# The last 512 gate columns of a decoder trunk: weight panels split ahead and kept, products token tile by token tile, the second tile in two halves

## Chip, cores, metric

One core of a Trainium2 chip. The time is device microseconds of one execution; several executions are timed and their median is given. One execution is also profiled, with a record of every instruction and DMA; its own time is given beside its span (first to last instruction). All durations below come from that profile.

## The reference

One layer of a decoder trunk for 256 tokens and a width of 2048, all in float32: a mixer (pooling and a recurrent time mix), a squared-ReLU MLP, and a gated embedding, then a final norm. The change touches the end alone:

```python
x = x + jnp.square(jax.nn.relu(h2 @ w_ffn_up[i])) @ w_ffn_down[i]
gate = jax.nn.sigmoid(rms_norm(x, ple_norm[i]) @ w_ple_gate[i])   # 2048 x 2048
x = x + gate * (p[i] @ w_ple_proj[i])                             # p: 256 wide
...
return rms_norm(x, final_norm)
```

## The kernel before, in words

**Numbers.** A float32 matrix product is made of three products of rounded operands: every operand v is split into a high part h (v rounded to float32r by a copy on ACT) and a low part l = v - h (a subtraction on DVE), and h·h + h·l + l·h is accumulated in PSUM. So weights can't go from memory straight to PE. A *panel* is 256 rows by 512 columns of a weight, 512 KB in SBUF as [128, 1024]. `load_raw` (L120) loads it on SP's DMA queue into one of three buffers `raw`; `split_w` (L125) makes `wh` (two ACT copies of 512 columns, L131; three buffers) and `wl` (one DVE subtraction, L132; two buffers). Then PE runs 12 matmuls with it: two row blocks, two token tiles of 128 tokens (tt = 0, 1), three products each (L153, L154, L155 in `prod_toks`). The activations are the stationary operand, the weights the moving one.

**Queues.** Every engine runs its instructions in one order, which the framework's scheduler sets from the order in the source and from priorities: the splits carry a high priority, so that they come as early in ACT's and DVE's order as their buffers let them. A load waits for its `raw` buffer (the split of three panels before), `wh` for PE's last matmul on the panel three before, `wl` for the one two before.

**The stages at the end**, all with `gemm_toks` (L172), which takes two PSUM banks from a ring of four (`mm_bank`), one for each token tile:
- the second half of the FFN's down product, tiles `d`, 4 column blocks of 16 panels. After each block DVE adds the result to the residual x, one operation for each token tile (L874), and PE transposes the new 512 columns into the banks `h3t` (L815), from which ACT and DVE make the split operand `h` of the gate product (L821, L822);
- the projection of p, tiles `pp`, 4 blocks of one panel each; ACT copies every bank to SBUF (L890). Beside it ACT sums the squares of x for the norm (L194, `junk`);
- the gate product, tiles `gt`, 4 column blocks n of 8 panels. After each block, for each token tile: sigmoid from the bank on ACT (L903), times pp (L908) and plus x (L909) on DVE, square with accumulation on ACT (L910), times the final norm's weights on DVE (L912, not in the last block);
- after the last block a sum of the accumulators (L914), root (L203) and reciprocal (L204) for both token tiles at once, then the scaling of x: ACT 768 columns (L919), DVE 768 (L920) and 512 (L921), and one store on ACT's queue (L922, 384 KB) and one on SP's (L923, 640 KB) for each token tile. A tiny activation `warm` (L906) makes ACT load the root's table early.

The FFN's activations stand in eight buffers `y` of [128, 2048], free once the last down block has used them.

## Time and profile before

| | |
|---|---|
| median of 3 runs (lowest to highest) | 1243.79 us (1243.69 to 1247.84) |
| the profiled execution, its span | 1242.95 us, 1241.2 us |
| granted TensorE clock, mean | 0.99 |
| ACT copy of 128x512 in a split (L131), gate panels | 624 ns |
| DVE subtraction of 128x1024 (L132), gate panels | 1224 ns |
| load of a gate panel, issue to landing, median | 3.5 us |
| PE's first and last matmul of the gate product | 1140 to 1227 us |

The rows of the profile read: start, duration, engine, source line, operation, output<-inputs, partitions x elements, and in brackets the idle time of the engine before it and what ended it. Rows of groups end in the busy time and the mean ns of one. A matmul's printed duration is from its issue to its end in a pipeline, so that consecutive ones overlap; the distance of their starts is what PE spends on each.

### The profile page before, as it was taken

The numbers are of one execution on the slowest core, as the hardware profiler recorded it, in microseconds if no ns is written. First come the engines' busy times: TensorE is split into PE (matmuls) and PEld (weight loads), VectorE is DVE, ScalarE is ACT, GpSimd is POOL, SyncE is SP. The second block draws the span as 40 slices with busy tenths as digits, with TensorE's granted clock in tenths as the row PEclk, the third lists the DMA queues.
The fourth block names the chain that finished last, engine by engine and source line by source line (L and its number), as shares of the span: only waits on it lengthen the run. The fifth ranks groups of instructions, "written<-read, shape, count | busy, mean of one in ns | idle before, by whom it ended". The sixth has DMA issues, their size and how long they took to land. (4 is left out here: it accounts for less than half of the span.)

```text
span 1241.2 us, 18647 instructions
## 1 busy us (share of the span) xinstructions
PE 1208.0 (97%) x7230; PEld 1039.7 (84%) x7230; DVE 751.0 (61%) x919; ACT 631.4 (51%) x1164; POOL 9.8 (1%) x58
## 2 busy tenths in 40 slices
PE   6999999999999999999999999999999999999995
PEld 4999898989888888888888888888888888888884
DVE  2678978875665566666554444656656455445564
ACT  6755555464455545555444444445544444446553
POOL 2000000000000000000000000000000000000000
PEclk9999999999999999999999999999999999999998
DMA  6453433222556656666666666655656655655663
GB/s 273 166 167 130 153 121 137 69 96 92 192 190 182 211 189 192 191 191 189 192 198 188 197 192 189 187 187 185 188 187 188 198 187 188 189 188 192 193 198 118
DMA packets 59944, 218.99 MB, mean 176 GB/s; under 512 B 6672, under 2 KB 6928, under 8 KB 59216
## 3 DMA queue, kind: packets, MB, share of 16 engines
q1 hardware_dynamic: 59424, 216.95, 54.5%
q8 instruction: 56, 0.92, 0.3%
q10 hardware_dynamic: 432, 0.86, 0.2%
q14 instruction: 32, 0.26, 0.1%
HBM read 215.68 MB, written 2.10 MB: 175 GB/s over the span
## 5 line engine op out<-in xcount | busy, mean ns | idle before, releaser
L794 PE MATMUL u_w<-h,wh_u 128*128 128x512 f32 x1024 | 358.8, 396 | 0.0
L798 PE MATMUL u_w<-h,wl_u 128*128 128x256 f32 x1024 | 285.6, 279 | 0.0
L132 DVE TENSOR_TENSOR wl_d<-raw_d,wh_d 128x1024 fp32r<-128x1024 f32 x128 | 156.7, 1224 | 163.6 <-PE d_b L154 149.4
L131 ACT ACTIVATE wh_d<-raw_d 128x512 fp32r<-128x512 f32 x256 | 147.6, 624 | 189.4 <-PE d_b L155 171.8
L131 ACT ACTIVATE wh_u<-raw_u 128x512 fp32r<-128x512 f32 x256 | 147.7, 625 | 175.6 <-PE u_w L794 145.8
L794 PEld LDWEIGHTS u_w<-h,wh_u 128*128 128x128 f32 x1024 | 192.2, 188 | 46.1
L132 DVE TENSOR_TENSOR wl_u<-raw_u,wh_u 128x1024 fp32r<-128x1024 f32 x128 | 156.6, 1223 | 117.7 <-PE u_w L798 111.7
L153 PE MATMUL d_b<-wh_d,y 128*128 128x512 f32 x512 | 199.8, 390 | 0.0
L155 PE MATMUL d_b<-wh_d,y 128*128 128x512 f32 x512 | 199.6, 390 | 0.0
L154 PE MATMUL d_b<-wl_d,y 128*128 128x512 f32 x512 | 199.2, 389 | 0.0
L798 PEld LDWEIGHTS u_w<-h,wl_u 128*128 128x128 f32 x1024 | 192.9, 188 | 0.0
L155 PEld LDWEIGHTS d_b<-wh_d,y 128*128 128x128 f32 x512 | 96.1, 188 | 20.0
L154 PEld LDWEIGHTS d_b<-wl_d,y 128*128 128x128 f32 x512 | 96.1, 188 | 19.9
L153 PEld LDWEIGHTS d_b<-wh_d,y 128*128 128x128 f32 x512 | 96.1, 188 | 19.5
L132 DVE TENSOR_TENSOR wl_gt<-raw_gt,wh_gt 128x1024 fp32r<-128x1024 f32 x32 | 39.2, 1224 | 33.8 <-PE gt_b L154 28.3
L131 ACT ACTIVATE wh_gt<-raw_gt 128x512 fp32r<-128x512 f32 x64 | 36.8, 624 | 29.6 <-PE gt_b L155 26.8
L153 PE MATMUL gt_b<-wh_gt,h 128*128 128x512 f32 x128 | 49.8, 389 | 0.0
L154 PE MATMUL gt_b<-wl_gt,h 128*128 128x512 f32 x128 | 49.8, 389 | 0.0
L155 PE MATMUL gt_b<-wh_gt,h 128*128 128x512 f32 x128 | 49.8, 389 | 0.0
L131 ACT ACTIVATE wh_o<-raw_o 128x512 fp32r<-128x512 f32 x48 | 27.7, 624 | 25.8 <-PE o_b L155 14.6
L144 PE MATMUL zk_b<-hTh,wh_zk 128*128 128x256 f32 x128 | 37.1, 291 | 2.8 <-ACT wh_zk L131 2.8
L146 PE MATMUL zk_b<-hTh,wl_zk 128*128 128x256 f32 x128 | 37.4, 292 | 2.1 <-DVE wl_zk L132 2.0
(337 smaller groups left out, 1975.7 us busy)
## 6 DMA issues: line engine op xcount, KB each, us to landing
raw_u<-in_w_ffn_up_dram SPq DMA_DIRECT2D x128, 512.0 KB, 3.5
raw_d<-in_w_ffn_down_dram SPq DMA_DIRECT2D x128, 512.0 KB, 3.5
raw_gt<-in_w_ple_gate_dram SPq DMA_DIRECT2D x32, 512.0 KB, 3.5
raw_o<-in_w_out_dram SPq DMA_DIRECT2D x24, 512.0 KB, 3.6
raw_zk<-in_w_in_dram SPq DMA_DIRECT2D x16, 512.0 KB, 3.4
raw_zr<-in_w_in_dram SPq DMA_DIRECT2D x16, 512.0 KB, 3.4
raw_zv<-in_w_in_dram SPq DMA_DIRECT2D x16, 512.0 KB, 3.5
raw_zp<-in_w_in_dram SPq DMA_DIRECT2D x16, 512.0 KB, 3.5
```

Source lines behind the costliest of these rows:

```text
L131: nc.scalar.activation(wh[:, a * 512 : (a + 1) * 512], raw[:, a * 512 : (a + 1) * 512], AF.Copy)
L132: nc.vector.tensor_tensor(wl, raw, wh.bitcast(F32), op=ALU.subtract)
L144: nc.tensor.matmul(o, w_h, ah, start=first and ct % 2 == 0, stop=False, skip_group_check=True)
L146: nc.tensor.matmul(o, w_l, ah, start=False, stop=last, skip_group_check=True)
L153: nc.tensor.matmul(o, a_h, wh[:, 0:n], start=first, stop=False)
L154: nc.tensor.matmul(o, a_h, wl[:, 0:n], start=False, stop=False)
L155: nc.tensor.matmul(o, a_l, wh[:, 0:n], start=False, stop=last)
L794: nc.tensor.matmul(bank[:, ct, :].rearrange("p (s t) -> p s t", s=2), wh[:, c], hl, start=k == 0, stop=False, skip_group_check=True,)
L798: nc.tensor.matmul(bank[:, ct, 0:T], wl[:, c], hl[:, 0, :], start=False, stop=k == 15, skip_group_check=True)
```

## The change

The last block of the gate product (n = 3) no longer streams its panels. Its eight panels are loaded and split earlier by `keep`, and both parts of each stay in a `y` buffer (`gk0` to `gk7`): two of them before panels 9 and 13 of the last FFN down block, one after each of the projection blocks 1 and 3, and one before panels 2 and 6 of the gate blocks 0 and 1. The last block is then computed from them in three runs: all 16 row blocks of token tile 0 (512 columns, bank `gt3a`), then of token tile 1 the first 256 columns (`gt3b`) and the second 256 (`gt3c`). Each run is followed by its own epilogue (`gated`), and token tile 0 is normed, scaled and stored (`final`) while token tile 1 is still multiplied. For 256 columns the epilogue writes the product into the other half of its buffer. A tile is stored in three parts of 512, 768 and 768 columns.

```diff
-    def split_w(raw, name):
+    def split_w(raw, name, into=None):
-        wh = wp.tile([128, 1024], F32R, tag="wh", name=f"wh_{name}")
-        wl = wp.tile([128, 1024], F32R, tag="wl", bufs=2, name=f"wl_{name}")
+        if into is None:
+            wh = wp.tile([128, 1024], F32R, tag="wh", name=f"wh_{name}")
+            wl = wp.tile([128, 1024], F32R, tag="wl", bufs=2, name=f"wl_{name}")
+        else:
+            wh, wl = into[:, 0:1024], into[:, 1024:2048]
...
-    def gemm_toks(src, acts, name, kps=None):
+    def gemm_toks(src, acts, name, kps=None, hooks=()):
...
+        hooks = dict(hooks)
         for i, kp in enumerate(kps):
+            if kp in hooks:
+                hooks[kp]()
             raw = load_raw(src[kp].rearrange("p a n -> p (a n)"), 1024, f"{name}_{kp}")
...
+    kept = []
+    def keep():
+        kp = len(kept)
+        raw = load_raw(w_gate[3, kp].rearrange("p a n -> p (a n)"), 1024, f"gk_{kp}")
+        kept.append(split_w(raw, f"gk_{kp}", fp.tile([128, 2048], F32R, tag="y", bufs=8, name=f"gk{kp}")))
...
-            banks = gemm_toks(w_down[n, hf * 16 : hf * 16 + 16], act, f"d{hf}_{n}")
+            ahead = {9: keep, 13: keep} if (hf, n) == (1, 3) else {}
+            banks = gemm_toks(w_down[n, hf * 16 : hf * 16 + 16], act, f"d{hf}_{n}", hooks=ahead)
...
             nc.scalar.activation(pp[tt][:, n * 512 : (n + 1) * 512], banks[tt], AF.Copy)
+        if n % 2:
+            keep()
...
-    for n in range(4):
-        banks = gemm_toks(w_gate[n], h3, f"gt{n}")
...
+    def gated(tt, n0, n, slot, src, last=False):
+        ns = slice(n0, n0 + n)
+        g_ = fp.tile([128, 512], F32, tag="r", bufs=2, name=f"gate{n0}{tt}")
+        gt, pr = g_[:, 0:n], g_[:, 512 - n : 512]
+        nc.scalar.activation(gt, src, AF.Sigmoid, scale=rs3[:, tt : tt + 1])
+        if last:
+            nc.scalar.activation(warm, gt[:, 0:1], AF.Sqrt)
+        nc.vector.tensor_tensor(pr, gt, pp[tt][:, ns], op=ALU.mult)
+        nc.vector.tensor_tensor(xr[tt][:, ns], xr[tt][:, ns], pr, op=ALU.add)
+        nc.scalar.activation(pr, xr[tt][:, ns], AF.Square, accum_out=ss4[:, tt, slot : slot + 1])
+        if not last:
+            nc.vector.tensor_tensor(xr[tt][:, ns], xr[tt][:, ns], fn[:, ns], op=ALU.mult)
+    for n in range(3):
+        banks = gemm_toks(w_gate[n], h3, f"gt{n}", hooks={kp: keep for kp in ((2, 6) if n < 2 else ())})
         for tt in range(2):
+            gated(tt, n * 512, 512, n, banks[tt])
+    def kept_product(tt, c0, n, name):
+        bank = mm_bank(name)
+        o, ts_ = bank[:, 0:n], slice(tt * 128, (tt + 1) * 128)
+        for k in range(NK):
+            hl = h3(k)
+            a_h, a_l = hl[:, 0, ts_], hl[:, 1, ts_]
+            wh, wl = (w[:, c0 : c0 + n] for w in kept[k // 2][k % 2])
+            nc.tensor.matmul(o, a_h, wh, start=k == 0, stop=False)
+            nc.tensor.matmul(o, a_h, wl, start=False, stop=False)
+            nc.tensor.matmul(o, a_l, wh, start=False, stop=k == NK - 1)
+        return o
+    def final(tt, slots, cut):
...
+        nc.scalar.activation(x_[:, 0:512], x_[:, 0:512], AF.Copy, scale=sc)
+        nc.scalar.dma_start(row[:, 0:512], x_[:, 0:512])
+        nc.vector.tensor_scalar_mul(x_[:, 512:1280], x_[:, 512:1280], sc)
+        nc.sync.dma_start(row[:, 512:1280], x_[:, 512:1280])
+        nc.scalar.activation(x_[:, 1280:cut], x_[:, 1280:cut], AF.Copy, scale=sc)
+        if cut < 2048:
+            nc.vector.scalar_tensor_tensor(x_[:, cut:2048], x_[:, cut:2048], sc, fn[:, cut:2048], op0=ALU.mult, op1=ALU.mult)
+        nc.sync.dma_start(row[:, 1280:2048], x_[:, 1280:2048])
+    gated(0, 1536, 512, 3, kept_product(0, 0, 512, "gt3a"))
+    final(0, 4, 2048)
+    gated(1, 1536, 256, 3, kept_product(1, 0, 256, "gt3b"))
+    gated(1, 1792, 256, 4, kept_product(1, 256, 256, "gt3c"), last=True)
+    final(1, 5, 1792)
```

Where the instructions stand now. First the loads on SP, from the last FFN down block (`d1_3`) to the projection (`pp0` to `pp3`), before:

```order
L122 DMA raw_d1_3_12_9975<-in_w_ffn_down_dram 128x1024
L122 DMA raw_d1_3_13_9994<-in_w_ffn_down_dram 128x1024
L122 DMA raw_d1_3_14_10013<-in_w_ffn_down_dram 128x1024
L122 DMA raw_d1_3_15_10032<-in_w_ffn_down_dram 128x1024
L122 DMA raw_pT_10070<-in_pT_dram 128x512
L122 DMA raw_pp0_0_10080<-in_w_ple_proj_dram 128x1024
L122 DMA raw_pp1_0_10103<-in_w_ple_proj_dram 128x1024
L122 DMA raw_pp2_0_10126<-in_w_ple_proj_dram 128x1024
L122 DMA raw_pp3_0_10149<-in_w_ple_proj_dram 128x1024
```

and with the change:

```order
L122 DMA raw_d1_3_12_9981<-in_w_ffn_down_dram 128x1024
L122 DMA raw_gk_1_10000<-in_w_ple_gate_dram 128x1024
L122 DMA raw_d1_3_13_10006<-in_w_ffn_down_dram 128x1024
L122 DMA raw_d1_3_14_10025<-in_w_ffn_down_dram 128x1024
L122 DMA raw_d1_3_15_10044<-in_w_ffn_down_dram 128x1024
L122 DMA raw_pT_10082<-in_pT_dram 128x512
L122 DMA raw_pp0_0_10092<-in_w_ple_proj_dram 128x1024
L122 DMA raw_pp1_0_10115<-in_w_ple_proj_dram 128x1024
L122 DMA raw_gk_2_10136<-in_w_ple_gate_dram 128x1024
L122 DMA raw_pp2_0_10144<-in_w_ple_proj_dram 128x1024
L122 DMA raw_pp3_0_10167<-in_w_ple_proj_dram 128x1024
L122 DMA raw_gk_3_10188<-in_w_ple_gate_dram 128x1024
```

Each kept panel takes its turn in the ring of three raw buffers: `d1_3_15` now gets the buffer that `gk1` leaves, and `pp2` comes behind `gk2`.

Then DVE at the start of the projection, where `x0` and `x1` are the residual of the two token tiles, before:

```order
L132 TENSOR_TENSOR wl_pp0_0_10083<-raw_pp0_0_10080,wh_pp0_0_10082 128x1024
L874 SCALAR_TENSOR_TENSOR x0_3586<-d1_3_b0_9745,s2sq_4339,x0_3586 128x512
L132 TENSOR_TENSOR wl_pp1_0_10106<-raw_pp1_0_10103,wh_pp1_0_10105 128x1024
L874 SCALAR_TENSOR_TENSOR x1_3587<-d1_3_b1_9746,s2sq_4339,x1_3587 128x512
L132 TENSOR_TENSOR wl_pp2_0_10129<-raw_pp2_0_10126,wh_pp2_0_10128 128x1024
```

and with the change:

```order
L135 TENSOR_TENSOR wl_pp0_0_10095<-raw_pp0_0_10092,wh_pp0_0_10094 128x1024
L889 SCALAR_TENSOR_TENSOR x0_3586<-d1_3_b0_9745,s2sq_4339,x0_3586 128x512
L135 TENSOR_TENSOR wl_pp1_0_10118<-raw_pp1_0_10115,wh_pp1_0_10117 128x1024
L135 TENSOR_TENSOR gk2_10138<-raw_gk_2_10136,gk2_10138 128x1024
L889 SCALAR_TENSOR_TENSOR x1_3587<-d1_3_b1_9746,s2sq_4339,x1_3587 128x512
L135 TENSOR_TENSOR wl_pp2_0_10147<-raw_pp2_0_10144,wh_pp2_0_10146 128x1024
```

The subtraction of the kept panel `gk2` stands between that of `pp1` and the second residual, for which the last transposes wait.

Last ACT at the end of the program, before:

```order
L903 ACTIVATE gate30_10840<-gt3_b0_10686,rs_n3_10183 128x512
L903 ACTIVATE gate31_10842<-gt3_b1_10687,rs_n3_10183 128x512
L906 ACT_TABLE_LOAD
L906 ACTIVATE warm_10187<-gate31_10842 128x1
L910 ACTIVATE gate30_10840,ss4_10186<-x0_3586 128x512
L910 ACTIVATE gate31_10842,ss4_10186<-x1_3587 128x512
L203 ACTIVATE rs_nf_10853<-ss_f_10851,eps_n_72 128x2
L919 ACTIVATE x0_3586<-x0_3586,rs_nf_10853 128x768
L919 ACTIVATE x1_3587<-x1_3587,rs_nf_10853 128x768
```

and with the change, from the store of token tile 0:

```order
L956 DMA out_0_dram<-x0_3586 128x512
L920 ACT_TABLE_LOAD
L920 ACTIVATE gate15361_10849<-gt3b_10800,rs_n3_10207 128x256
L925 ACTIVATE gate15361_10849,ss4_10210<-x1_3587 128x256
L920 ACTIVATE gate17921_10904<-gt3c_10855,rs_n3_10207 128x256
L922 ACT_TABLE_LOAD
L922 ACTIVATE warm_10211<-gate17921_10904 128x1
L925 ACTIVATE gate17921_10904,ss4_10210<-x1_3587 128x256
L951 ACTIVATE rsf1_10912<-ssf1_10910,eps_n_72 128x1
L955 ACTIVATE x1_3587<-x1_3587,rsf1_10912 128x512
L959 ACTIVATE x1_3587<-x1_3587,rsf1_10912 128x512
L956 DMA out_0_dram<-x1_3587 128x512
```

Token tile 0 is scaled and stored ahead of both halves of token tile 1, and the sigmoid's table is loaded once more between them. Lines of the changed kernel are some 3 higher at L131 to L155 (L134 to L158) and 15 higher at L874 (L889).

31 lines of the change are left out of this document (7 added, 24 removed).

## The prediction

> **What bounds the kernel now.** I read the page's first lines, then the windows of the end of the program, then the timelines of the two places that the change touches.
>
> ```profile
> PE 1208.0 (97%) x7230; PEld 1039.7 (84%) x7230; DVE 751.0 (61%) x919; ACT 631.4 (51%) x1164; POOL 9.8 (1%) x58
> 1129.00:1141.00 12.00, 11.61 (x55) 9.30 (x54) 7.47 (x10) 12.00 (x26) 0.00 (x0) 1.00 0.54 169
> 1141.00:1170.00 29.00, 29.00 (x130) 24.01 (x129) 16.88 (x19) 17.00 (x32) 0.00 (x0) 1.00 0.60 196
> 1227.00:1241.20 14.20, 0.64 (x3) 0.19 (x1) 5.56 (x10) 6.24 (x11) 0.00 (x0) 0.59 0.36 148
> ```
>
> The columns after a window are its length and then PE, PEld, DVE, ACT, POOL busy, granted clock, DMA share, GB/s. PE is busy everywhere but at the ends, so two things can change the time: work added to or stalls put into the PE stream, and the last 14.2 us, where PE does nothing. The second row is the stage of the projection (pp): there ACT is busy for 12.00 of 12.00 us, so it has no room. In the gate stage (third row) ACT has 12 us free in 29 and DVE 12.
>
> The tail after the last product, as its chain runs now:
>
> ```profile
> 1226.57 0.39 PE L155 MATMUL gt_b<-wh_gt,h 128*128 128x512 f32 x1
> 1227.25 0.39 PE L155 MATMUL gt_b<-wh_gt,h 128*128 128x512 f32 x1
> 1227.67 0.69 ACT L903 ACTIVATE gate<-gt_b,rs_n 128x512 f32<-128x512 f32 x1
> 1228.38 1.28 ACT L906 ACT_TABLE_LOAD   x1
> 1229.78 0.61 ACT L910 ACTIVATE gate<-x 128x512 f32<-128x512 f32 x1
> 1229.91 0.69 DVE L908 TENSOR_TENSOR gate<-gate,pp 128x512 f32<-128x512 f32 x1 [0.78 <-ACT warm L906]
> 1230.64 0.69 DVE L909 TENSOR_TENSOR x<-x,gate 128x512 f32<-128x512 f32 x1
> 1231.42 0.63 ACT L910 ACTIVATE gate<-x 128x512 f32<-128x512 f32 x1 [0.93 <-DVE x L909]
> 1231.96 0.19 ACT L910 ACTIVATION_READ_ACCUMULATOR gate<-x 128x1 f32 x1
> 1232.90 0.62 DVE L920 TENSOR_SCALAR x<-x,rs_nf 128x768 f32<-128x768 f32 x1
> 1234.63 0.75 DVE L921 SCALAR_TENSOR_TENSOR x<-x,rs_nf,fn 128x512 f32<-128x512 f32 x1
> 1235.40 0.34 SPq L923 DMA_DIRECT2D out_dram<-x  x1
> L923 SPq DMA_DIRECT2D out_dram<-x x2: 344/346/348, 1234.2 to 1235.4; - x2
> DMA to landing us min/median/max: 3.6/4.2/4.8
> L922 ACTq DMA_DIRECT2D out_dram<-x x2: 338/341/344, 1233.9 to 1234.7; - x2
> DMA to landing us min/median/max: 2.5/3.3/4.1
> ```
>
> Call S the start of token tile 1's sigmoid (1227.67) and Z the start of the final scaling (1232.90). S to Z is 5.23 us: sigmoid, table load, then a multiply that waits for the warm activation (it overwrites what that reads), add, square, and 0.75 from the accumulator's end (1232.15) through reduce, root and reciprocal. From Z it takes 2.50 to the last store's issue, 4.8 to its landing (1240.2), 1.0 to the span's end (1241.2): 8.30.
>
> **Part 1, the tail (a gain).** Only the last 256 columns of one tile come behind the last matmul. The ACT price of 256 columns less comes from these rows:
>
> ```profile
> L194 ACT ACTIVATE junk_n<-x 128x1024 f32<-128x1024 f32 x3 | 3.2, 1052 | 0.0
> L910 ACT ACTIVATE gate<-x 128x512 f32<-128x512 f32 x8 | 5.0, 629 | 5.3 <-DVE x L909 5.3
> L822 DVE SCALAR_TENSOR_TENSOR h<-h3t,par_sb,h 128x256 fp32r<-128x256 f32 x4 | 1.9, 482 | 2.1 <-ACT h L821 2.1
> ```
>
> 512 columns cost 1052 - 629 = 423 ns, so 256 cost 0.21 us. Sigmoid: 0.69 - 0.21 + 0.02 to the next = 0.50. Table load to square is 1229.78 - 1228.38 = 1.40. The multiply and add on DVE, under 0.48 each by the last row, end by 0.50 + 0.96 = 1.46, inside those 1.90, and they write the other half of the buffer, so nothing waits for the warm activation. Square and accumulator, 0.73 now (1231.42 to 1232.15), take 0.52; then the same 0.75. S to Z becomes 3.17: **-2.06**.
>
> After Z the second tile alone is scaled: on ACT two copies of 512 columns, on DVE 768 and 256.
>
> ```profile
> 1146.12 1.15 ACT L131 ACTIVATE wh_gt<-raw_gt 128x512 fp32r<-128x512 f32 x2 [1.57 <-PE gt_b L155]
> 1234.10 0.62 DVE L920 TENSOR_SCALAR x<-x,rs_nf 128x768 f32<-128x768 f32 x1
> ```
>
> The ACT pair takes 1.15, so the last stores are issued at Z + 1.25 (now Z + 2.50), and 384 KB already at Z + 0.65. Now 384 KB land first at 1233.9 + 2.5 = 1236.4, and the other 1664 KB by 1240.2, 438 KB per us. So 384 KB land at Z + 3.15 and the remaining 640 KB 1.46 later, Z + 4.6; plus 1.0 is 5.6 in place of 8.30: **-2.7**. Ends: if the last store needs 4.8 as now, 1.25 + 4.8 + 1.0 = 7.05 (-1.25); if only 2.5, 4.75 (-3.55).
>
> Tile 0's own tail hides behind tile 1's products (about 11.5 us). Its chain is S to Z without a separate wait, about 4.8, two copies of 512 and 768 columns (0.6 + 0.9 by the L919 row's 1.76 for two) and a sigmoid table again (1.28): ACT is free some 7.6 us after tile 0's sigmoid starts, finishes the first half's epilogue by 9.3, and the second half's sigmoid is due at 11.5. Cover 2 us. Without it every us goes straight to the end.
>
> **Part 2, the products (a loss).** 48 matmuls of 512 columns become 96 of 256.
>
> ```profile
> 185.76 0.28 PE L144 MATMUL zp_b<-hTh,wh_zp 128*128 128x256 f32 x1
> 185.88 0.28 PE L145 MATMUL zp_b<-hTl,wh_zp 128*128 128x256 f32 x1
> 499.69 0.40 PE L794 MATMUL u_w<-h,wh_u 128*128 128x512 f32 x1
> 499.92 0.28 PE L798 MATMUL u_w<-h,wl_u 128*128 128x256 f32 x1
> 500.04 0.39 PE L794 MATMUL u_w<-h,wh_u 128*128 128x512 f32 x1
> ```
>
> What counts is start to start, not the 0.28 to 0.40 of one. Three matmuls of 512 take 1227.25 - 1226.57 = 0.68, so 0.227 each; one of 256 takes 0.12. 96 x 0.12 - 48 x 0.227 = **+0.64**; in the FFN rows 256 columns take 0.12 too, so I take no other value than +0.64, with +0.2 as the low end (0.115, the start to start that the printed hundredths still allow). The Trainium skill, "TensorE: Matmul & The Clock Gate", section "Back-to-back issue gap", gives N/2.4 + 2.5 ns for an isolated gap, 215.8 and 109.2 ns; by that the halves would cost an estimated 96 x 0.1092 - 48 x 0.2158 = +0.12, and the rows here differ from it (227 and 120). The last matmul, shorter by 0.11 (0.39 to 0.28), lets S come 0.11 earlier: **-0.11**.
>
> **Part 3, splitting ahead (a loss).** Eight panels' loads, 16 ACT copies and 8 DVE subtractions move from the last gate columns to earlier panels: two to the last FFN product, two to pp, four to gate columns 0 and 1. Their number is unchanged. A panel occupies PE 12 x 0.227 = 2.72 us, and in the steady stages ACT idles 1.57 of it (1146.12 row) while an inserted split needs 1.15, so the four in the gate stage and most of the two in the FFN hide behind matmuls. In pp nothing hides them:
>
> ```profile
> L122 SPq DMA_DIRECT2D raw_pp<-in_w_ple_proj_dram x4: 328/328/328, 1121.1 to 1127.2; - x4
> DMA to landing us min/median/max: 3.5/4.3/5.0
> 1127.54 2.39 ACT L131 ACTIVATE wh_pp<-raw_pp 128x512 fp32r<-128x512 f32 x4 [1.66 <-DMA raw_pp<-in_w_ple_proj_dram]
> 1128.72 1.22 DVE L132 TENSOR_TENSOR wl_pp<-raw_pp,wh_pp 128x1024 fp32r<-128x1024 f32 x1 [0.52 <-ACT wh_pp L131]
> 1129.87 0.74 DVE L874 SCALAR_TENSOR_TENSOR x<-d_b,s2sq,x 128x512 f32<-128x512 f32 x1
> 1129.88 0.40 PE L155 MATMUL pp_b<-wh_pp,pl 128*128 128x512 f32 x1
> 1130.67 0.33 PE L815 MATMUL h3t<-ident,x 128*128 128x128 f32 x1 [0.39 <-DVE x L874]
> ```
>
> PE already waits here: its transposes come 0.79 after the matmul before, 0.56 more than a matmul's 0.227, because tile 1's residual (L874) stands on DVE behind the second projection panel's subtraction, whose load took 5.0. In the new order a kept panel stands between those two. Following the rows of the new order with these durations: (a) the load of the last FFN panel is issued one subtraction later (1.2), since the kept panel took a slot of the ring of three and its own subtraction runs first; PE waits for that panel and for the second projection panel some **0.6** in sum; (b) the residual runs one subtraction later still (1.15 start to start) and the transposes wait **1.3** more; (c) two ACT splits, 2.3 us, enter a stretch where ACT is full, so that its copies of the projection banks, for which PE waits before it may reuse a bank, come later: **1.7** of the 2.3, the rest falling into (b)'s wait. Sum **+3.6**. Ends: 0 if loads and bank copies have slack that I don't see; 8 x 1.15 = 9.2 if every inserted split holds PE for its whole ACT time.
>
> **Sum** against the profiled execution (1242.95 beside a span of 1241.2): -2.06 - 2.7 + 0.64 - 0.11 + 3.6 = -0.6. The median of the runs shown is 1243.79, 0.84 above that execution, so I forecast **1243.2**.
>
> **Rivals.**
> - *The stall doesn't come* (part 3 at 0 to 1): -4.2 to -3.2, so about 1240.0. For it: PE waits only 0.39 in pp now although ACT is full, so ACT's backlog has some slack. Against it: the order rows put the kept subtraction directly ahead of the residual. With stores at their best too (-3.55) and the low end of part 2, -4.2 - 0.85 - 0.44 = -5.5, 1238.3: hardly past 0.5%.
> - *Every insertion stalls* (slower): the ring of three raw buffers is the place. If loads land 5.0 after issue wherever a ninth comes between eight, as in pp, and not 3.5, each insertion holds PE for its split: 9.2 - 4.2 = +5.0, and with the stores at 4.8 +6.4, 1250.2. It decides once part 3 passes 4.2. Against it: in the steady stages ACT idles 1.57 waiting for PE, not for DMA.
> - *The clock falls*. At the program's start a wait of PE was followed by half clock:
>
> ```profile
> 30.00:32.00 2.00, 0.40 (x2) 0.40 (x3) 2.00 (x3) 2.00 (x5) 0.00 (x0) 0.50 0.30 84
> 32.00:34.00 2.00, 2.00 (x11) 2.00 (x11) 2.00 (x3) 1.13 (x2) 0.00 (x0) 0.50 0.65 234
> ```
>
>   PE was busy for 0.40 of 2 us, and the 2 us after it, full of work, ran at 0.50. If pp's waits did that, 4 us of matmuls at half speed cost about +2 more: 1245.2. My longest wait is 0.56 + 1.3, under 2 us, so I give it little. The Trainium skill, same page, section "What's actually happening", has the clock halved after an idle window of about 3.4 us; by that it would not fall here, and the windows above agree.
> - *The change doesn't do what it says*: the order rows have the split-ahead panels and the halves where the words put them, so no chance is kept for it.
>
> **How the numbers follow.** About 0.5% (6.2 us) is what a measurement of this kernel can tell from no change. Forecast, between -3 and +3: 0.50. No stall: 0.24. Every insertion stalls: 0.20. Clock: 0.06. Past -6.2 lies a quarter of the no-stall case (stores and stalls both beyond my ends) and a little of the rest: faster 0.08. Past +6.2 lies most of the slower rival and a part of the clock's: slower 0.16. Same: 0.76. The range for 8 in 10 runs from the no-stall case, 1238.8, to the bound of the slower rival less a little, 1249.5; the forecast's own is 1240 to 1246.
>
> **What would show it.** Right: last matmul to span's end near 9 us (14 now); 256-column matmuls 0.12 apart; L889's second tile just before a PE wait of about 2 us at h3t, and PE waiting for ACT's pp copies; gate stage without PE waits. Wrong: PE idle under 1 us between the last FFN product and the gate columns (then the no-stall rival), waits of PE on wl_gt or wl_d at each kept panel (the slower rival), a granted clock under 1.00 in pp, a last sigmoid that starts later than 0.4 after its last matmul, or stores landing over 4 us after issue.

## The result: 3.4 us slower, and where it went

The changed kernel takes 1247.12 us (median of 20 runs, 1241.64 to 1253.99), the kernel before beside it 1243.74 us (20 runs, 1239.4 to 1250.52): a ratio of 1.0026, 95% interval 1.0014 to 1.0039. That is slower, by half of what was called distinguishable from no change, where -0.6 us was forecast. The profiled execution of the changed kernel took 1248.2 us, its span 1246.4.

The first lines of its page give engine, busy time, share of the span, instructions:

```profile
PE 1213.7 (97%) x7278; PEld 1041.8 (84%) x7278; DVE 751.6 (60%) x924; ACT 636.3 (51%) x1172; POOL 9.8 (1%) x58
```

Nothing stands out there: PE has its 48 further matmuls, and all else is as before. The difference is read from the windows of the end of the program, cut at the start of the first matmul of each stage: projections, gate blocks 0 to 2, last block with tail. (The FFN's last products, where two of the panels ahead stand, take 177.1 us in both kernels.) Columns as in the prediction. Before:

```profile
1127.70:1140.40 12.70, 12.31 (x58) 9.85 (x57) 7.72 (x10) 12.62 (x25) 0.00 (x0) 1.00 0.55 171
1140.40:1205.70 65.30, 65.30 (x289) 54.05 (x289) 36.90 (x38) 35.54 (x67) 0.00 (x0) 1.00 0.61 195
1205.70:1241.20 35.50, 21.94 (x97) 17.83 (x95) 17.70 (x23) 15.19 (x29) 0.00 (x0) 0.84 0.37 130
```

and with the change:

```profile
1129.60:1144.50 14.90, 13.21 (x58) 9.63 (x58) 10.41 (x12) 12.44 (x25) 0.00 (x0) 1.00 0.77 233
1144.50:1214.80 70.30, 67.11 (x289) 53.59 (x288) 40.94 (x43) 40.49 (x75) 0.00 (x0) 1.00 0.61 190
1214.80:1246.40 31.60, 22.55 (x145) 20.47 (x143) 10.27 (x21) 13.03 (x25) 0.00 (x0) 0.92 0.17 67
```

The last stage is 3.9 us shorter, the projections 2.2 longer, and the gate blocks 5.0 longer: 70.30 against 65.30, with PE busy for all of it before and idle for 3.2 us now. Neither ScalarE nor VectorE is full there (40.49 and 40.94 of 70.30), so it is not their total time that is short. The sum of the three is +3.3, close to the difference of the medians, 3.4. (The two profiled spans differ by 5.2, because two earlier stretches that the change does not touch differ too: what comes before the FFN by -1.4, the up-products of the FFN by +3.3; on them below.)

The waits of PE in projections and gate blocks name what ended last (total us, times, longest). Before there was one:

```profile
PE h3t L815 <- DVE x L874: 0.4, 1, 0.4
```

and now:

```profile
PE gt_b L157 <- DVE wl_gt L135: 2.1, 2, 1.3
PE h3t L821 <- DVE x L889: 1.1, 2, 0.9
PE gt_b L156 <- ACT pp L905: 0.9, 1, 0.9
PE pp_b L156 <- ACT pp L905: 0.4, 1, 0.4
PE pp_b L157 <- DVE wl_pp L135: 0.2, 1, 0.2
```

The last four are the stalls that were forecast around the projections. The first is not: PE waits for a split of the gate's own weights. The longest such wait, from the timelines of SP, ScalarE, VectorE and PE in the changed kernel (start, duration, instruction, in brackets the idle time before it and what ended it), in block 1, whose third panel is late:

```profile
1166.10 0.33 SPq L122 DMA_DIRECT2D raw_gk<-in_w_ple_gate_dram  x1
1168.11 1.15 ACT L134 ACTIVATE wh_gt<-raw_gt 128x512 fp32r<-128x512 f32 x2 [1.68 <-DMA raw_gt<-in_w_ple_gate_dram]
1170.60 1.15 ACT L134 ACTIVATE gk<-raw_gk 128x512 fp32r<-128x512 f32 x2 [1.34 <-DMA raw_gk<-in_w_ple_gate_dram]
1171.77 1.28 ACT L920 ACT_TABLE_LOAD   x1
1171.78 1.23 DVE L135 TENSOR_TENSOR gk<-raw_gk,gk 128x1024 fp32r<-128x1024 f32 x1 [1.25 <-ACT gk L134]
1173.06 0.69 ACT L920 ACTIVATE gate<-gt_b,rs_n 128x512 f32<-128x512 f32 x1
1173.65 1.15 ACT L134 ACTIVATE wh_gt<-raw_gt 128x512 fp32r<-128x512 f32 x2
1175.12 1.22 DVE L135 TENSOR_TENSOR wl_gt<-raw_gt,wh_gt 128x1024 fp32r<-128x1024 f32 x1
1176.39 0.50 PE L157 MATMUL gt_b<-wl_gt,h 128*128 128x512 f32 x1 [1.29 <-DVE wl_gt L135]
```

The copies on ScalarE are those of the block's second panel (1168.11), the kept one (1170.60) and the third (1173.65). ScalarE waits 1.68 us for the second panel to land and 1.34 for the kept one, then it has block 0's table load and sigmoid, and only then comes the third panel: 5.54 us after the second, where PE takes 2.72 for one. In the kernel before, the same two panels' copies lie 3.06 us apart, around the same table load and sigmoid; the 2.48 us between are the wait of 1.34 for the kept panel and its copies' own 1.15:

```profile
1159.67 1.15 ACT L131 ACTIVATE wh_gt<-raw_gt 128x512 fp32r<-128x512 f32 x2 [1.57 <-PE gt_b L155]
1160.85 1.28 ACT L903 ACT_TABLE_LOAD   x1
1162.14 0.69 ACT L903 ACTIVATE gate<-gt_b,rs_n 128x512 f32<-128x512 f32 x1
1162.73 1.14 ACT L131 ACTIVATE wh_gt<-raw_gt 128x512 fp32r<-128x512 f32 x2
```

There ScalarE's idle time ends with PE, which gives back a buffer; with the change it ends with a load. The view of the tile raw_gt adds that up over all its panels (32 before, 24 now): what ended the idle time of the splitting engines (us, times). Before:

```profile
  PE gt_b L155: 28.7, 21
  PE gt_b L154: 28.3, 20
  DMA raw_gt<-in_w_ple_gate_dram: 2.8, 1
```

and with the change:

```profile
  ACT wh_gt L134: 15.4, 13
  DMA raw_gt<-in_w_ple_gate_dram: 13.4, 14
  PE gt_b L157: 6.5, 5
```

Fourteen splits now start when their load lands, where one did. Why three buffers are short can be estimated from the kept panel's rows: a buffer was taken at 1166.10 and was free again when the subtraction ended, at 1171.78 + 1.23 = 1173.01, a turn of 6.9 us. Three buffers then bring a panel every 2.3 us. PE uses one in 2.72, so each panel leaves 0.4 us of slack, and a panel ahead, which takes 2.3, is made good after five or six others. The change puts one ahead of every fourth panel in the gate blocks, and two behind one another in the projections. By the same estimate, four buffers would bring a panel every 1.7 us.

The tail came as worked out. Its chain, with the second half of token tile 1 alone behind the last matmul:

```profile
1237.08 0.28 PE L943 MATMUL gt3c<-gk,h 128*128 128x256 f32 x1
1237.39 0.47 ACT L920 ACTIVATE gate<-gt3c,rs_n 128x256 f32<-128x256 f32 x1 [1.91 <-PE gt3c L943]
1239.29 0.40 ACT L925 ACTIVATE gate<-x 128x256 f32<-128x256 f32 x1
1240.53 0.72 ACT L955 ACTIVATE x<-x,rsf 128x512 f32<-128x512 f32 x1 [0.23 <-DVE rsf L952]
1241.89 0.33 SPq L962 DMA_DIRECT2D out_dram<-x  x1
```

From the sigmoid to the scaling 3.14 us (3.17 forecast), from there to the span's end 5.87 (5.6 forecast).

### The profile page after: what moved, and what is told of

Same layout as the page of the kernel before. It is cut to its first block, busy times and chain, and to the rows that moved or that the text cites. A ratio compares the mean times of both kernels' runs of the same rounds, so it can differ in the third digit from the quotient of the medians.

```text
span 1246.4 us, 18743 instructions
## 1 busy us (share of the span) xinstructions
PE 1213.7 (97%) x7278; PEld 1041.8 (84%) x7278; DVE 751.6 (60%) x924; ACT 636.3 (51%) x1172; POOL 9.8 (1%) x58
## 4 chain that ended last, share of the span: by engine, by line
PE 66%; DMA 3%; ACT 1%; DVE 1%; issue 0%; ACTq 0%; DVEq 0%
PE u_w L800 19%; PE u_w L804 10%; PE d_b L156 9%; PE d_b L158 9%; PE d_b L157 9%; PE o_b L158 1%; PE o_b L156 1%; PE o_b L157 1%; DMA raw_gt<-in_w_ple_gate_dram 1%; PE gt_b L157 1%; PE gt_b L158 1%; PE gt_b L156 1%; DMA raw_pp<-in_w_ple_proj_dram 1%; DVE wl_gt L135 1%; ACT wh_gt L134 0%; DMA raw_gk<-in_w_ple_gate_dram 0%
## 5 line engine op out<-in xcount | busy, mean ns | idle before, releaser
L134 ACT ACTIVATE wh_d<-raw_d 128x512 fp32r<-128x512 f32 x256 | 147.6, 624 | 186.1 <-PE d_b L158 160.1
L134 ACT ACTIVATE wh_u<-raw_u 128x512 fp32r<-128x512 f32 x256 | 147.7, 625 | 179.6 <-PE u_w L800 147.3
L158 PE MATMUL d_b<-wh_d,y 128*128 128x512 f32 x512 | 199.6, 390 | 0.0
L158 PEld LDWEIGHTS d_b<-wh_d,y 128*128 128x128 f32 x512 | 96.1, 188 | 20.1
L135 DVE TENSOR_TENSOR wl_gt<-raw_gt,wh_gt 128x1024 fp32r<-128x1024 f32 x24 | 29.4, 1224 | 21.8 <-ACT wh_gt L134 15.4
L134 ACT ACTIVATE wh_o<-raw_o 128x512 fp32r<-128x512 f32 x48 | 27.6, 624 | 25.7 <-PE o_b L158 15.0
L157 PE MATMUL gt_b<-wl_gt,h 128*128 128x512 f32 x96 | 38.0, 395 | 2.3 <-DVE wl_gt L135 2.1
L148 PE MATMUL zk_b<-hTl,wh_zk 128*128 128x256 f32 x128 | 37.9, 296 | 2.1 <-DVE hTl L140 2.1
L135 DVE TENSOR_TENSOR wl_o<-raw_o,wh_o 128x1024 fp32r<-128x1024 f32 x24 | 29.3, 1223 | 17.2 <-PE o_b L157 12.1
L156 PE MATMUL gt_b<-wh_gt,h 128*128 128x512 f32 x96 | 37.5, 391 | 0.9 <-ACT pp L905 0.9
```

Source lines behind the costliest of these rows:

```text
L134: nc.scalar.activation(wh[:, a * 512 : (a + 1) * 512], raw[:, a * 512 : (a + 1) * 512], AF.Copy)
L135: nc.vector.tensor_tensor(wl, raw, wh.bitcast(F32), op=ALU.subtract)
L148: nc.tensor.matmul(o, w_h, al, start=False, stop=False, skip_group_check=True)
L156: nc.tensor.matmul(o, a_h, wh[:, 0:n], start=first, stop=False)
L157: nc.tensor.matmul(o, a_h, wl[:, 0:n], start=False, stop=False)
L158: nc.tensor.matmul(o, a_l, wh[:, 0:n], start=False, stop=last)
```

## The experiments

For every kernel that ran, the profile was cut into the same stretches: the FFN from its first up-product's matmul to its last (both halves), from there to the last FFN matmul, projections, gate blocks 0 to 2, last block to its last matmul, tail from the start of that to the span's end. All are differences of two starts in one profiled execution, in us; the ratio to the kernel before is over all runs of both, 4 to 35 of each. What comes before the first up-product, which the change does not touch, is not in the table: it took 414.3 to 422.4 us in these 18 profiles, so whole spans of single executions say little about the change.

| kernel | up-products | last FFN products | projections | gate 0 to 2 | last block | tail | ratio (95%) |
|---|---|---|---|---|---|---|---|
| before | 533.3 | 177.1 | 12.7 | 65.3 | 21.5 | 14.0 | |
| changed | 536.6 | 177.1 | 14.9 | 70.3 | 22.3 | 9.4 | 1.0026 (1.0014 to 1.0039) |
| e4_neither | 536.9 | 177.1 | 12.6 | 65.3 | 22.3 | 9.3 | 0.9992 (0.9978 to 1.0006) |
| e2_loads | 536.6 | 177.2 | 14.7 | 69.9 | 22.3 | 9.4 | 1.0028 (1.0012 to 1.0045) |
| e3_small | 536.6 | 178.3 | 14.2 | 67.5 | 22.3 | 9.4 | 1.0039 (1.0024 to 1.0054) |
| e1_ownraw | 536.6 | 178.9 | 14.1 | 65.3 | 22.3 | 9.4 | 1.0013 (0.9999 to 1.0028) |
| p1_before_pad | 533.3 | 177.1 | 12.1 | 65.3 | 21.5 | 14.2 | 0.9999 (0.9982 to 1.0017) |
| p2_after_pad | 533.7 | 177.3 | 14.2 | 69.4 | 22.3 | 9.4 | 1.0020 (1.0002 to 1.0037) |
| p3_ring4 | 533.3 | 177.1 | 12.6 | 65.7 | 22.3 | 9.4 | 0.9979 (0.9959 to 0.9999) |
| p5_spread | 533.7 | 179.1 | 13.3 | 66.9 | 22.3 | 9.4 | 1.0005 (0.9985 to 1.0024) |
| q1_after_again | 533.3 | 177.4 | 14.5 | 69.0 | 22.3 | 9.4 | 1.0033 (1.0015 to 1.0050) |
| q2_before_pad5 | 536.6 | 177.1 | 12.3 | 65.3 | 21.5 | 14.2 | 1.0013 (0.9997 to 1.0029) |
| q3_neither_pad | 533.3 | 177.1 | 12.7 | 65.3 | 22.3 | 9.4 | 0.9948 (0.9932 to 0.9965) |
| q4_ring4_whole | 533.3 | 177.1 | 12.7 | 65.4 | 21.5 | 11.5 | 0.9977 (0.9957 to 0.9997) |
| r1_before_plain | 533.4 | 177.1 | 12.4 | 65.3 | 21.5 | 14.0 | 0.9997 (0.9984 to 1.0011) |
| r2_before_pad5 | 533.3 | 177.1 | 12.4 | 65.3 | 21.5 | 14.2 | 0.9997 (0.9983 to 1.0011) |
| r3_ring4_nopad | 536.8 | 177.1 | 12.6 | 66.0 | 22.3 | 9.4 | 0.9984 (0.9967 to 1.0000) |
| r4_before_pad3 | 533.4 | 177.2 | 12.4 | 65.3 | 21.5 | 14.2 | 1.0015 (1.0000 to 1.0029) |

The theory, A: the loads come late, because a panel ahead takes a turn in the ring of three. The rival, B: the time of the eight further splits on ScalarE and VectorE is what PE waits for.

### Loads and splits taken apart

**Neither** (e4_neither): no load and no split ahead; the last block multiplies FFN buffers that hold something else.

```diff
-        raw = load_raw(w_gate[3, kp].rearrange("p a n -> p (a n)"), 1024, f"gk_{kp}")
-        kept.append(split_w(raw, f"gk_{kp}", fp.tile([128, 2048], F32R, tag="y", bufs=8, name=f"gk{kp}")))
+        kept.append(None)
...
```

> The change without its splitting ahead: no kept panel is loaded or split, and the last block multiplies what stands in the FFN activation buffers (its output is not the reference's). Both theories (late loads; engine time) expect the projection stretch (last FFN matmul to first gate matmul) back at 12.7 us (14.9 with the change), the gate blocks 0 to 2 back at 65.3 (70.3), the last block and tail at 31.6 as with the change: in all 3.9 us under the kernel before, some 1240. If the stretches stay long, neither theory holds and the halves or the epilogues disturb them.

Projections and gate blocks are back at 12.6 and 65.3: all of what was lost there hangs on the panels ahead, and the new last block and tail alone give +0.7 and -4.6. The median fell by 0.5 us only, where 3.9 was expected. In the profiled execution the up-products took 3.5 longer, which would account for it if the other executions did the same. That was new, and the third group of runs is about it.

**The loads alone** (e2_loads): the loads stay at their places in the ring, no split follows.

```diff
-        raw = load_raw(w_gate[3, kp].rearrange("p a n -> p (a n)"), 1024, f"gk_{kp}")
-        kept.append(split_w(raw, f"gk_{kp}", fp.tile([128, 2048], F32R, tag="y", bufs=8, name=f"gk{kp}")))
+        load_raw(w_gate[3, kp].rearrange("p a n -> p (a n)"), 1024, f"gk_{kp}")
+        kept.append(None)
...
```

As in the run before, the last block multiplies FFN buffers.

> The eight kept panels are loaded at their places in the ring of three, but not split; the last block multiplies what stands in the FFN buffers (output not the reference's). Theory A (late loads: each extra 512 KB makes its neighbours land late): the gate blocks stay at 68 to 70 us, the projection stretch at 14 or more. Theory B (time on ACT and DVE for eight more splits): gate blocks 65.3 to 66, projection stretch 12.7 to 13.

Gate blocks 69.9, projections 14.7: nearly the whole loss without a single split ahead. But some 1.6 us of the gate blocks' 4.6 are half clock after one long wait (see the last section), which the changed kernel's gate blocks do not have; the waits themselves come to about 3.0. So late loads alone do most of the harm, and B as the only cause falls. That the splits' time adds nothing is not shown by this run.

**The splits with small loads** (e3_small): each load ahead brings 32 KB of its panel instead of 512; the splits read those columns over and over, so the last block's weights are others.

```diff
-        raw = load_raw(w_gate[3, kp].rearrange("p a n -> p (a n)"), 1024, f"gk_{kp}")
+        raw = load_raw(w_gate[3, kp, :, 0, 0:64], 64, f"gk_{kp}")
...
+                nc.scalar.activation(
+                    wh[:, a * 512 : (a + 1) * 512].rearrange("p (r c) -> p r c", c=64), r3.to_broadcast([128, 8, 64]), AF.Copy
+                )
...
```

> The eight kept panels are split at their places from their ring buffers, but only 32 KB of each are loaded (64 columns, read sixteen times over; the last block's weights are wrong). Order of all engines as with the change. Theory A (late loads): gate blocks 65.3 to 66.5 us, projection stretch about 13 to 14. Theory B (ACT and DVE time): gate blocks 69 to 70, projection stretch 14.9. If both this and the loads alone stay long, it is the turn in the ring of three buffers, not bytes or engine time.

Gate blocks 67.5, more than A's 66.5 and less than B's 69, and the last FFN products 1.2 longer. So 2.2 us of the 5.0 come without the bytes. A small load still takes its turn in the ring, and its buffer comes free only behind its split; whether the 2.2 are that turn or the splits' time, this run can't tell. The ring of four, below, has both the bytes and the splits.

**A raw buffer of their own** (e1_ownraw): the panels ahead no longer pass through the ring.

```diff
-        raw = load_raw(w_gate[3, kp].rearrange("p a n -> p (a n)"), 1024, f"gk_{kp}")
+        raw = fp.tile([128, 1024], F32, tag="rawk", bufs=1, name=f"rawk_{kp}")
+        nc.sync.dma_start(raw, w_gate[3, kp].rearrange("p a n -> p (a n)"))
```

> The kept panels get a raw buffer of their own beside the ring of three. The scheduler then takes all but one of them into the last FFN block and the projection, none into the gate blocks. Theory A and B: gate blocks 65.3 to 66.5 us. Theory A: the last FFN block, with up to 1.5 times the bytes, gets some stalls, 2 to 4 us, projection stretch 14 to 16; in all between the kernel before and the changed one, 1241 to 1246. Theory B: the FFN block, where ACT idles 1.57 us per panel, takes them free, projection stretch 14, in all 1240 to 1242.

Gate blocks 65.3, but the run tells less than it was meant to: freed of the ring, the order put all eight splits into the last FFN block (six) and the projections (two), which became 1.8 and 1.4 longer. The gate blocks had no panels ahead to suffer from.

### Four loads under way, and the panels spread

The next runs carry one unread constant, which shifts the buffers by 32 bytes (why, is told below). **The changed kernel with it** (p2_after_pad) is their reference:

> The changed kernel with the same extra constant, so that its buffers lie 192 bytes behind those of before (a multiple of 64, not of 128) instead of 160. Theory C: the up stretch falls from 536.6 to 533.3 us, gate blocks 0 to 2 stay at 69.5 to 70.5, tail at 9.3, and the total is 3.3 us under the changed kernel's: a ratio to before of 0.9990 to 1.0008. Theory D: 536.6 again, ratio 1.0026. If only multiples of 128 counted: 536.6 too, though the run with before's buffers moved is slow.

**A ring of four** (p3_ring4): from the last FFN block on, every fourth panel is loaded into a buffer in the FFN's pool. The source places the panels ahead where the change has them; in the trace one of their loads comes one panel later and the splits of the last three up to one panel earlier.

```diff
+    ring = [0, 0]
...
     def load_raw(src, n, name):
-        raw = wp.tile([128, 1024], F32, tag="raw", name=f"raw_{name}")
+        ring[1] += ring[0]
+        if ring[1] % 4 == 3:
+            raw = fp.tile([128, 1024], F32, tag="raw3", bufs=1, name=f"raw_{name}")
+        else:
+            raw = wp.tile([128, 1024], F32, tag="raw", name=f"raw_{name}")
...
+            if (hf, n) == (1, 3):
+                ring[0] = 1
```

> As the run before it (changed kernel with the extra constant), and from the last FFN block on every fourth panel is loaded into a fourth raw buffer in the FFN's pool, so that four loads may be under way instead of three; splits ahead stay where they are. Theory A (the loads come late, because a load ahead takes a turn in a ring of three): gate blocks 0 to 2 fall from 70.0 to 65.3 to 67.0 us, the stretch of the projections from 14.9 to 13 to 14; total 1239 to 1242. Theory B (time of the splits on ScalarE and VectorE): gate blocks stay at 69 to 70.5. A third, A2 (the transfers themselves share the DMA engines, so that more of them under way land later each): 68 to 70, and the median landing of the gate panels rises above 4.4 us.

Its windows of projections and gate blocks:

```profile
1132.20:1144.80 12.60, 12.53 (x58) 9.70 (x57) 8.94 (x10) 12.29 (x26) 0.00 (x0) 1.00 0.76 261
1144.80:1210.50 65.70, 65.62 (x290) 53.99 (x289) 41.01 (x43) 38.42 (x73) 0.00 (x0) 1.00 0.60 190
```

VectorE does as much in the gate blocks as in the changed kernel (41.01 against 40.94), and PE is idle for 0.08 us there instead of 3.2. The view of raw_gt has the splits waiting for PE again:

```profile
  PE gt_b L163: 13.6, 10
  PE gt_b L164: 7.7, 7
  issue: 6.5, 6
  DVE wl_gt L141: 2.5, 1
  DMA raw_gt<-in_w_ple_gate_dram: 2.2, 3
```

The loads of the gate's own panels did not become quicker: the median landing is 4.4 us here as in the changed kernel. They are only asked for earlier: from a load's issue to its panel's first matmul it is 11.0 us in the median, against 8.1 in the changed kernel and 9.6 in the kernel before. That settles A against B, and against A2, that transfers crowd each other: with all loads and all splits ahead, 3.8 of the 4.2 us over 65.3 in the gate blocks go with one more buffer, and the projections are back where they were. The total is 1239.18 us against 1242.37 for the kernel before beside it (0.9979, an interval that ends at 0.9999), and 0.4% under the same kernel with three buffers.

**The panels spread** (p5_spread), with three buffers: four in the last FFN block, none in the projections, four over three gate blocks.

```diff
-            ahead = {9: keep, 13: keep} if (hf, n) == (1, 3) else {}
+            ahead = dict.fromkeys((5, 8, 11, 14), keep) if (hf, n) == (1, 3) else {}
...
-        if n % 2:
-            keep()
...
-        banks = gemm_toks(w_gate[n], h3, f"gt{n}", hooks={kp: keep for kp in ((2, 6) if n < 2 else ())})
+        banks = gemm_toks(w_gate[n], h3, f"gt{n}", hooks=dict.fromkeys(((4,), (3, 6), (4,))[n], keep))
```

> As the second run (changed kernel with the extra constant), but the eight panels ahead are spread: four in the last FFN block (ahead of its panels 5, 8, 11 and 14), none in the projections, one in gate block 0 (ahead of panel 4), two in block 1 (3 and 6), one in block 2 (4). Theory A: a load ahead costs where two come within 6 panels of each other or next to a block's end, so gate blocks 0 to 2 take 66.5 to 68.5 us, the projections 12.7 to 13.2, the last FFN block at most 1 us more; total 1238.5 to 1241. Theory B (each split costs its 1.2 us wherever it stands in the gate stage): gate 69.5 to 70, projections 12.7, total 1241 to 1243.

Gate blocks 66.9 and projections 13.3 are about A's figures; the last FFN block is 2.0 longer where at most 1 was expected, so the total is no better than that of the kernel before (1243.18 against 1242.37). The waits of PE in this kernel:

```profile
PE d_b L157 <- DVE wl_d L135: 1.3, 2, 1.0
PE gt_b L157 <- DVE wl_gt L135: 0.9, 1, 0.9
```

One ahead of every third panel is more than three buffers bear in the FFN as well; two, four panels apart, as in the change, were hidden there.

**Four buffers, the second tile whole** (q4_ring4_whole): what the halves are worth. The edit is to the ring of four.

```diff
-    gated(1, 1536, 256, 3, kept_product(1, 0, 256, "gt3b"))
-    gated(1, 1792, 256, 4, kept_product(1, 256, 256, "gt3c"), last=True)
-    final(1, 5, 1792)
+    gated(1, 1536, 512, 3, kept_product(1, 0, 512, "gt3b"), last=True)
+    final(1, 4, 1536)
```

> The kernel with four loads under way in the gate stage (the third run of the batch before), but the second token tile is one run of 512 columns instead of two halves. The halves cost 96 matmuls of 256 columns against 48 of 512, +0.8 us measured over the last block, and shorten the sigmoid, the two products and the square behind the last matmul by 0.2 to 0.3 us each. Expected: last block 21.4 to 21.6 us, tail from the last matmul's start 10.1 to 10.5, together within 0.4 us of the halves; gate blocks 65.3 to 66.0; total ratio to before 0.997 to 0.999.

The last block is 0.7 shorter, about as expected, but the tail 2.2 longer instead of about 1: by the stretches the halves bring 1.4 us. The ratios do not show it (0.9977 here, 0.9979 for the ring of four with the halves, both intervals 0.0040 wide). The expectation missed a wait. Its timeline behind the last matmul, on ScalarE and VectorE:

```profile
1229.64 0.69 ACT L930 ACTIVATE gate<-gt3b,rs_n 128x512 f32<-128x512 f32 x1 [3.23 <-PE gt3b L953]
1230.34 1.28 ACT L932 ACT_TABLE_LOAD   x1
1231.87 0.69 DVE L933 TENSOR_TENSOR gate<-gate,pp 128x512 f32<-128x512 f32 x1 [7.70 <-ACT warm L932]
1233.38 0.63 ACT L935 ACTIVATE gate<-x 128x512 f32<-128x512 f32 x1 [1.54 <-DVE x L934]
```

With 512 columns the product overwrites what the warm activation reads, and waits for it and for the table load before it; with 256 it writes the other half of the buffer and starts as soon as the sigmoid is done, 0.51 us after the sigmoid's start at 1237.39. In the changed kernel:

```profile
1237.90 0.42 DVE L923 TENSOR_TENSOR gate<-gate,pp 128x256 f32<-128x256 f32 x1 [1.96 <-ACT gate L920]
```

**Neither, with the constant** (q3_neither_pad): what the new last block and tail give alone.

> Neither loads nor splits ahead (the last block multiplies FFN buffers that are there anyway, so its output isn't the reference's), with one extra constant: buffers 192 bytes behind before's. What is left of the change is its last block and tail: -4.7 at the end and +0.8 in the last block, so -3.9 +- 0.5 by the stretches, 1238.0 to 1239.0, ratio 0.9965 to 0.9972, if the up stretch is 533.3 (theories C2 and E on a quick chip); about -0.6 if it is 536.6 here (theory E on a slow one, before then being slow too would give -3.9 all the same).

The stretches gave -3.9 us (+0.7 and -4.6) as expected, the total 1238.24 against 1243.75, ratio 0.9948 (0.9932 to 0.9965), beyond the 0.9965 to 0.9972 that was expected. Some 1.6 us of the 5.5 are thus not explained by the stretches that the change touches, and stay open. This is the floor that a cost-free splitting ahead would reach; the ring of four is 0.3 us above it by its stretches, but 0.0031 above it by the ratios, 3.9 us, measured on another chip.

### The up-products

In the changed kernel and its first four variants the up-products took 536.6 to 536.9 us, in the kernel before 533.3, with the same instructions in the same order. It is all in the FFN's first half. These are the groups of the two matmul shapes in 40 us of that half (count, busy, mean ns), in the kernel before:

```profile
L794 PE MATMUL u_w<-h,wh_u 128*128 128x512 f32 x116 | 40.3, 394 | 0.0
L798 PE MATMUL u_w<-h,wl_u 128*128 128x256 f32 x116 | 32.1, 277 | 0.0
```

and in the changed one:

```profile
L800 PE MATMUL u_w<-h,wh_u 128*128 128x512 f32 x114 | 40.3, 399 | 0.0
L804 PE MATMUL u_w<-h,wl_u 128*128 128x256 f32 x114 | 32.0, 281 | 0.0
```

No wait, a granted clock of 1.00, and each matmul 4 to 5 ns longer. One thing that differs for these instructions is where their operands lie: by the count of the change's small constants, all buffers behind them are moved by 160 bytes. Hence the runs with unread constants (**p1_before_pad**, one, 32 bytes; **q2_before_pad5** and **r2_before_pad5**, five, 160; **r4_before_pad3**, three, 96), the changed kernel again (**q1_after_again**), the kernel before again (**r1_before_plain**), and the ring of four without the constant (**r3_ring4_nopad**).

```diff
     warm = const.tile([128, 1], F32, name="warm")
+    for i in range(5):
+        pad = const.tile([128, 1], F32, name=f"pad{i}")
+        nc.gpsimd.memset(pad, 0.0)
```

> The kernel before, with one more constant of 4 bytes a partition (a tile 'pad' that is set to zero and never read), which moves every buffer allocated behind it by 32 bytes: the weight and activation tiles of the matmuls then begin at 32 bytes past a multiple of 64, as they do in the changed kernel and in its four variants, where before they begin at a multiple of 64. Theory C (the address of the operands sets the pace of the up-products): the stretch of the FFN's up-products and its first half, first u matmul to last, is 536.6 +- 0.4 us instead of 533.3, all other stretches as before, the total about +3.3 us, ratio 1.0027. Theory D (something else in the changed kernels slows them, such as their code or the buffers shared with the kept panels): 533.3, ratio 1.000.

> The changed kernel once more, unaltered, beside the next run on one chip. The up stretch was 536.6 us in its first profile and in four variants that ran on one other chip, 533.3 in four kernels on a third chip. Theory C2 (buffers that begin 160 bytes further are read more slowly): 536.6 again. Theory E (the pace of that stretch differs from chip to chip, or from one execution to the next, whatever the kernel): the same figure as in the next run and in the third on this chip, whichever it is. Gate blocks 70 +- 0.7, projections 14 to 15, total 1.0014 to 1.0039 of before by either.

> The kernel before with five constants of 4 bytes that are set to zero and never read, 32 bytes each, so that all matmul operands from the FFN on lie 160 bytes further, exactly where the changed kernel has them. Theory C2: up stretch 536.6 us, all others as before, total +3.3 us, ratio 1.0027. Theory E: the up stretch equals that of the run before and of the next, and the ratio is 0.999 to 1.001.

> The kernel before, unaltered (buffers at offset 0), for a second profile of it. First half's up stretch 533.3 us (from the first u matmul to the last, both halves) by every theory but E, which allows 536.6 in some executions of any kernel. Ratio 0.999 to 1.001.

> The kernel before with five unread constants again (buffers 160 bytes further). Theory C3 (at this offset the stretch falls into the slower pace in most executions): 536.6 us, ratio 1.001 to 1.003. Theory E (chance, the same for every offset): 533.3 as likely as in the run before; ratio 0.999 to 1.001.

> The changed kernel with four loads under way in the gate stage, without the extra constant, so with buffers 160 bytes further. Gate blocks 65.3 to 66.0, projections 12.5 to 13, tail 9.3, as with the constant. C3: up stretch 536.6, ratio 0.9985 to 1.0005. E: 533.3 as likely as in the first run; ratio 0.996 to 0.999.

> The kernel before with three unread constants (buffers 96 bytes further, like 160 no multiple of 64). C3: 533.3 if only 160 is concerned, 536.6 if offsets of 32 over a multiple of 64 are (against the one run with 32). E: as the others. Ratio 0.999 to 1.003.

No theory held. A fixed effect of the address falls: the same kernel at 160 bytes took 536.6 (q2_before_pad5) and 533.3 (r2_before_pad5), the changed one 536.6 and 533.3 (q1_after_again). Offsets of 32 and 96 were quick, so it is not the remainder against 64 either. But pure chance is hard to believe too: 536.6 or more came in seven of nine profiles at 160 bytes and in none of nine at other offsets (0, 32, 96, 192). Nor is it the chip: 536.6 of q2_before_pad5 and 533.3 of q1_after_again were taken on one. Over all runs the effect of 160 bytes on the kernel before cannot be told from nothing (1.0013 and 0.9997, both intervals hold 1). But the kernel with neither loads nor splits ahead is 0.9992 (0.9978 to 1.0006) at 160 bytes and 0.9948 (0.9932 to 0.9965) at 192, two intervals that lie apart; the two were measured on different chips. What sets the pace is open.

That the change is slower does not hang on it: with the constant, where the up-products were quick, the changed kernel (p2_after_pad) is still at 1.0020 (1.0002 to 1.0037). The ring of four is ahead of the kernel before at both offsets, 0.9979 with the constant and, with an interval that ends at 1.0000, 0.9984 without.

How much of the 3.4 us the change itself costs is less certain. Of its three profiles, the stretches that the change touches add up to +3.3 in the first, +1.9 in the second (q1_after_again: 0.3, 1.8, 3.7, 0.7 and -4.6) and +1.9 with the constant, where the medians differ by 3.4, 3.6 and 1.8: the gate blocks alone vary by up to 1.3 us from one execution of the same kernel to the next. So by the stretches the change itself costs 1.9 to 3.3 us; whether the rest is up-products in the slower pace, no run here shows.

## Why the prediction failed

Point by point, by its own terms:

- **Part 1, the tail**: held. -2.06 forecast for sigmoid to scaling, -2.09 measured (5.23 to 3.14); -2.7 for what follows, -2.43 measured (8.30 to 5.87); the last matmul's -0.11 came exactly (0.42 to 0.31 from its start to the sigmoid).
- **Part 2, the products**: held, +0.7 over the last block (21.5 to 22.3) against +0.64.
- **Part 3, around the projections**: held in sum, 3.3 against 3.6. The projections are 2.2 longer, and the first wait in the gate blocks, 1.33 us from one matmul's start (1145.18) to the next (1146.51) instead of 0.23, is still ScalarE's late copies of the projection banks (term c), 1.1. By terms it is less even: (c) came to 1.7 as forecast (this wait, and 0.80 instead of 0.23 from 1138.74 to 1139.54); (a), the waits ahead of the residual, to 0.8 against 0.6 (matmuls that start at 1129.86, 1130.43 and 1131.09); (b), the transposes' longer wait, only to 0.5 against 1.3 (1.33 from 1133.80 to 1135.13, where it was 0.79). The remaining 0.3 is in smaller steps.
- **Part 3, the gate stage**: failed. The step is "in the steady stages ACT idles 1.57 of it (1146.12 row) while an inserted split needs 1.15, so the four in the gate stage and most of the two in the FFN hide behind matmuls". It was put at nothing and measured +3.9 (5.0 less the 1.1 above). The row it rests on is right, and ScalarE did have the room; what it lacked was the panel. The step priced the split of a moved panel and not its load, though term (a) of the same part counts the lost turn in the ring for the last FFN panel. In the two FFN places nothing was lost, as said.

With that term the sum is -2.09 - 2.43 - 0.11 + 0.7 + 3.3 + 3.9 = +3.3, against 3.4 between the medians. That the two come so close is in part luck: the other two profiles of the changed kernel give +1.9.

The rival "every insertion stalls" named the place, the ring of three, and the point from which it decides, part 3 past 4.2; part 3 came to 7.2. Its mechanism was the right one, with loads of 4.4 us in the median instead of the 5.0 it assumed, though not every insertion stalled. It had 0.20, and the argument against it, that ScalarE waits for PE and not for a load, described the state without insertions: one wait for a load in 32 panels there, 14 in 24 in the changed kernel. The clock did not fall in the changed kernel's projections and gate blocks, whose longest gap between matmul starts was 1.67 us; the rival's price did not arise. The prediction's remark that its windows of the program's start agree with an idle window of about 3.4 us is not borne out, though: there PE's last matmul ended at 25.93 us (L294), the granted clock was still 1.00 from 26 to 28 us and 0.54 from 28 to 30, so some 2.2 us without a matmul came before half clock.

## What to carry to other kernels

A panel that is moved into a steady stage brings its load with it: before its split is called hidden, count the turns in the ring of raw buffers from its issue to its landing, and see whether the engine's idle time still ends with the consumer and not with a load. Where it ended with a load, one more buffer of 512 KB in the ring was worth 5 us here (1244.13 to 1239.18), and moving the panels about 1 us (1243.18). Where the engine that splits also runs an epilogue, a late panel queues behind that too, as at the turn of the first two gate blocks here.

## What the hardware showed beside

**A gap of 2.6 us brought half clock, and one of 2.3 us did in some executions.** In the run with the loads alone, PE waited once for 2.25 us, and its matmuls after that started 0.43 us apart instead of 0.227. The matmul after the gap, which followed one that started at 1174.75, and then the windows around it (the granted clock is the third number from the end):

```profile
1177.39 0.66 PE L157 MATMUL gt_b<-wl_gt,h 128*128 128x512 f32 x1 [2.25 <-DVE wl_gt L135]
```

```profile
1172.00:1174.70 2.70, 2.70 (x13) 2.16 (x12) 0.68 (x2) 0.99 (x2) 0.00 (x0) 1.00 0.70 226
1177.40:1180.80 3.40, 3.40 (x8) 2.67 (x9) 1.68 (x2) 0.77 (x2) 0.00 (x0) 0.53 0.59 159
1181.20:1184.60 3.40, 3.40 (x17) 2.81 (x16) 1.37 (x2) 1.15 (x2) 0.00 (x0) 1.00 0.77 255
```

Eight matmuls in 3.4 us instead of some 15 to 17, about 1.6 us on top of the wait. The Trainium skill, "TensorE: Matmul & The Clock Gate", section "What's actually happening", puts the half clock behind an idle window of about 3.4 us that runs freely. The length of the slow stretch agrees with that figure, the length of the gap does not: 2.6 us without a matmul's start were enough here. Nor does the length alone decide. Every one of the 18 profiles has a gap of 2.3 us between matmul starts near 126 us, in a part that the change does not touch. In six of them half clock followed within 1.4 us of the gap's end and lasted 3.4: in the changed kernel's first profile the gap is 2.29 us from 125.8, and the granted clock from 128.4 to 131.6 is 0.50. In the other twelve no half clock followed within 20 us: in the same kernel's second profile (q1_after_again) the gap is 2.29 us from 127.3, and the clock from 129.8 to 132.8 is 1.00. So these runs give no length of gap that is safe or that is too long; the changed kernel's gaps of up to 1.7 and 2.1 us in the last stages of those two profiles passed at full clock, and that may have been luck.

**One stage with two paces.** The 3.3 us of the up-products, above: the same matmuls, no waits, full clock, mean durations of 399 and 281 ns in some executions and 394 and 277, or 391 and 280, in others. A difference of this size between two profiles is thus not a cost of a change until it has been seen in more than one execution.
